# Layer A's queries and keys turned in 32 by 32 blocks by VectorE, with the quadrants moved by ScalarE, instead of by TensorE transposes

## The chip, the cores and the metric

The kernel runs on one core of a Trainium2 chip. The metric is device time in microseconds (us), from the start of the program to its end. Comparisons are made between medians of several runs. The profile is of one further execution, with every engine's instructions recorded. Its engines are PE (TensorE, matmuls) with PEld (its weight loads), DVE (VectorE), ACT (ScalarE), POOL (GpSimd) and SP (SyncE, which issues the weight loads from memory).

## The reference

Two layers over 256 tokens of width 2048, all in float32. Layer A (the first) is the one concerned:

```
xn   = rms_norm(h, norm_attn[0]);  mem_n = rms_norm(mem, norm_mem[0])
proj = xn @ w_in_a[0]                       # 12 heads of q, k, v, then 4 heads of qm, 128 wide each
q = rms_norm(split_heads(proj[q part], 12), qk_gain_a[0, 0])     # norm over each head's 128
k = rms_norm(split_heads(proj[k part], 12), qk_gain_a[0, 1])
v = split_heads(proj[v part], 12)
y_main = chunk_band_attention(q, k, v, rel_bias[0])              # softmax over the band, with bias
y_mem  = memory_attention(split_heads(proj[qm part], 4), mem_n, w_mem_kv[0], ...)
h = h + concat(y_main, y_mem) @ w_o[0]
h = h + square(relu(rms_norm(h, norm_mlp[0]) @ w_mlp_in[0])) @ w_mlp_out[0]
```

Layer B uses stick-breaking attention in place of the band attention, and is not touched. Scores are products of queries and keys over the 128 of a head, so both must lie with those 128 on the partitions, while the norm over a head is a sum along the 128 for each token.

## The kernel before

**Products in two parts.** Every weight is split into a high part `hi`, rounded to PE's fast float32 format, and a rest `lo`; activations are split in the same way. A product is three matmuls: hi by hi, hi by lo, lo by hi. The weights come as a `stream` of units of 128 partitions by 1024. For each unit SP loads `raw` (L250), ACT casts it to `hi` (L170), and DVE subtracts to get `lo` (L173). The pools hold 6 raw, 4 hi and 5 lo buffers. `weights` (L254) keeps `AHEAD` = 3 further units prepared in the code's order, so a unit's cast stands in the code three units before its matmuls.

**Layer A's projections.** `tokens_major` (L314) makes 512 columns of a projection for all 256 tokens, in two accumulator banks, one for each half of 128 tokens. It goes through 8 weight units of 12 matmuls (`tile_by_tokens`, L291), and the matmul's output has tokens on the partitions. There are ten such calls in layer A (L1203 to L1222): qm, the queries of the memory attention, and then for each of three groups of four heads the queries q, the keys k and the values v.

**Slots and side work.** Attention runs beside the projections. After each unit, `slot` (L271) advances a clock and lets each active generator take one step; a `yield` ends a step. `queue_side` (L268) puts a generator into a first-in first-out line, from which `slot` starts one at the earliest 5 slots after it was queued and `gap` slots after the one before it. Only PE's instructions are kept in the order of the code (`InOrder`, L64), with a few pinned ones; the other engines' instructions are ordered by the framework's scheduler, and each engine then executes its own in that order.

**What makes a normed query or key.** When the eighth unit is through, `normed_heads` (L553) is called. For each half of the tokens `half` (L556) squares the bank on ACT (L558), sums over each head on DVE (L560, L564), takes the inverse root on POOL (L568), and multiplies on DVE into `qn` (L570), a tile of 128 tokens by four heads of 128. After `wait` = 2 slots a side generator turns it: for each half, one slot apart, four PE transposes of 128x128 into a PSUM tile `tp` (L586), and one ACT activation of 128x512 (L589) that multiplies by the gain, one factor per partition, and writes the half's 128 columns of each head in `dst`.

**Who reads it.** `mem_head` (L641) multiplies queries by memory keys into `s` (L646), takes a softmax on ACT and DVE, transposes the probabilities on PE into `tp`, copies them on ACT to `pt` (L628), multiplies with the values into `yp`, and splits the result (L470, L471). `band_head` (L664) loads a bias on SP's queue and fills a corner of it on POOL, and one slot later does the same with q and k of its own group. Four memory heads are queued after qm with a gap of 4, and four band heads after each k group with a gap of 2, 2 and 1 (L1206, L1216).

Of the kernel before, what the change touches and what calls it, by code (L numbers as in the profile page):

```python
# [9 lines left out]
F32 = mybir.dt.float32  # L10
F32R = mybir.dt.float32r
AF = mybir.ActivationFunctionType
# [4 lines left out]
P = 128  # L17
D = 2048
T = 256
# [3 lines left out]
HD = 128  # L23
# [9 lines left out]
G_QK = 7 * 16  # L33
# [69 lines left out]
def trunk(  # L103
# [17 lines left out]
    nc = Engines(tc)  # L121
# [7 lines left out]
    wide = ctx.enter_context(tc.tile_pool(name="wide", bufs=7))  # L129
# [15 lines left out]
    sm = const.tile([P, N_SMALL], F32, name="sm")  # L145
# [115 lines left out]
    waiting = deque()  # L261
    active = []
    clock = {"slot": 0, "last": -99}
# [1 line left out]
    def start_side(g):  # L265
        active.append(g)

    def queue_side(g, gap):  # L268
        waiting.append((g, gap, clock["slot"] + 5))

    def slot():  # L271
        clock["slot"] += 1
        if waiting and clock["slot"] >= max(clock["last"] + waiting[0][1], waiting[0][2]):
            active.append(waiting.popleft()[0])
            clock["last"] = clock["slot"]
        for g in list(active):
            try:
                next(g)
            except StopIteration:
                active.remove(g)  # L280
# [28 lines left out]
    def unit_by_tokens(banks, act, half):  # L309
        unit = weights()  # L310
        for k2 in range(2):
            tile_by_tokens(banks, act, unit, k2, 2 * half + k2)

    def tokens_major(act, evacuate):  # L314

        banks = [ps_mm.tile([P, 512], F32, name="acc", tag="acc") for _ in range(2)]
        width["last"] = "wide"
        for half in range(8):
            unit_by_tokens(banks, act, half)
            if half == 7:  # L320
                evacuate(banks)
            slot()
# [227 lines left out]
        nc.vector.reciprocal(r2[:], r2[:])  # L550
        return r2

    def normed_heads(banks, eps_ms, gain, dst, wait=2):  # L553


        def half(m):  # L556
            sq = wide.tile([P, 512], F32, name="sqw", tag="wide")
            nc.scalar.activation(sq[:], banks[m][:], AF.Square)  # L558
            ss = tiny.tile([P, 4], F32, name="ss", tag="t4", bufs=8)
            nc.vector.tensor_reduce(  # L560
                ss[:], sq[:].rearrange("p (h d) -> p h d", d=HD), AX.X, ALU.add
            )
            ms = tiny.tile([P, 4], F32, name="msq", tag="t4", bufs=8)
            nc.vector.tensor_scalar(  # L564
                ms[:], ss[:], 1.0 / HD, eps_ms[:, 2 * m : 2 * m + 1], op0=ALU.mult, op1=ALU.add
            )
            s = tiny.tile([P, 4], F32, name="sroot", tag="t4", bufs=8)
            nc.gpsimd.tensor_tensor(s[:], ms[:], neg_half[:], op=ALU.pow)  # L568
            qn = wide.tile([P, 512], F32, name="qn", tag="wide")
            nc.vector.tensor_tensor(  # L570
                qn[:].rearrange("p (h d) -> p h d", d=HD),
                banks[m][:].rearrange("p (h d) -> p h d", d=HD),
                s[:].unsqueeze(2).to_broadcast([P, 4, HD]),
                op=ALU.mult,
            )
            return qn

        def side():
            qns = [half(0), half(1)]
            for _ in range(wait):  # L580
                yield
            for m in range(2):
                yield
                tp = ps_t.tile([P, 512], F32, name="tp", tag="t")
                for j in range(4):
                    nc.tensor.transpose(  # L586
                        tp[:, j * P : (j + 1) * P], qns[m][:, j * P : (j + 1) * P], ident[:]
                    )
                nc.scalar.activation(  # L589
                    dst.rearrange("p (h t) -> p h t", t=T)[:, :, m * P : (m + 1) * P],  # L590
                    tp[:].rearrange("p (h t) -> p h t", t=P),
                    AF.Copy,
                    scale=gain,
                )

        g = side()
        next(g)
        start_side(g)
# [42 lines left out]
    def mem_head(qm, km, vm, j, y, lag):  # L641
        s = ps_s.tile([P, 512], F32, name="s", tag="s")
        k = km[:, j * T : (j + 1) * T]
        for m in range(2):
            q = qm[:, j * T + m * P : j * T + (m + 1) * P]
            mm(s[:, m * T : (m + 1) * T], q, k, True, True)  # L646
        nmax = tiny.tile([P, 2], F32, name="nmax", tag="t2", bufs=8)
        nc.vector.tensor_reduce(
            nmax[:], s[:].rearrange("p (m k) -> p m k", k=T), AX.X, ALU.max, negate=True
        )  # L650
        p = wide.tile([P, 512], F32, name="p", tag="wide")
        sums = tiny.tile([P, 2], F32, name="sums", tag="t2", bufs=8)
        for m in range(2):
            nc.scalar.activation(
                p[:, m * T : (m + 1) * T], s[:, m * T : (m + 1) * T], AF.Exp,
                bias=nmax[:, m : m + 1], accum_out=sums[:, m : m + 1],
            )
        rs = tiny.tile([P, 2], F32, name="rs", tag="t2", bufs=8)
        nc.vector.reciprocal(rs[:], sums[:])
        for _ in range(lag):  # L660
            yield
        yield from soft_tail(p, [(0, T), (T, 2 * T)], rs, vm, j, y, NH + j, None, lag)

    def band_head(qt, kt_, vt, j, head, y, ready, lag):  # L664
        bias = nar.tile([P, T], F32, name="bias", tag="bias", bufs=6)
        nc.sync.dma_start(
            bias[:],
            bass.AP(tensor=rel.tensor, offset=rel.offset + head * REL + 129, ap=[[1, P], [1, T]]),
        )
        nc.gpsimd.memset(bias[0:64, 0:64], MASKED)  # L670
        yield
        s = ps_s.tile([P, 512], F32, name="s", tag="s")
        q0 = qt[:, j * T : j * T + P]
        q1 = qt[:, j * T + P : (j + 1) * T]
        mm(s[:, 0:P], q0, kt_[:, j * T : j * T + P], True, True)
        mm(s[:, P : P + T], q1, kt_[:, j * T : (j + 1) * T], True, True)
        ns = wide.tile([P, 512], F32, name="ns", tag="wide")
        nmax = tiny.tile([P, 2], F32, name="nmax", tag="t2", bufs=8)
        for m, (lo, hi) in enumerate([(0, P), (P, P + T)]):
            n = hi - lo  # L680
            nc.vector.tensor_tensor_reduce(
                out=ns[:, lo:hi], in0=s[:, lo:hi], in1=bias[:, n - 1 :: -1] if n < T else bias[:, ::-1],
                scale=-1.0, scalar=-MASKED, op0=ALU.add, op1=ALU.min,
                accum_out=nmax[:, m : m + 1],
            )
        p = ns
        sums = tiny.tile([P, 2], F32, name="sums", tag="t2", bufs=8)
        for m, (lo, hi) in enumerate([(0, P), (P, P + T)]):
            nc.scalar.activation(
                p[:, lo:hi], ns[:, lo:hi], AF.Exp, bias=nmax[:, m : m + 1], scale=-1.0,  # L690
                accum_out=sums[:, m : m + 1],
            )
        rs = tiny.tile([P, 2], F32, name="rs", tag="t2", bufs=8)
        nc.vector.reciprocal(rs[:], sums[:])
        for _ in range(lag):
            yield
        yield from soft_tail(p, [(0, P), (P, P + T)], rs, vt, j, y, head, ready, lag)
# [190 lines left out]
    gq = const.tile([P, 3], F32, name="gq")  # L888
# [8 lines left out]
    mstat = {}  # L897
    xg = None
# [8 lines left out]
    km, vm = [], []  # L907

    for l, mg in enumerate((mg0, mg1)):
        if l == 1:  # L910
            xg = new_act("xg")
# [3 lines left out]
        k_ = heads4(f"km{l}")  # L915
        km.append(k_)
        vm.append(heads4(f"vm{l}"))
        g = G_QK + 2 * (1 + l) + 1
# [281 lines left out]

    start_side(x_stat_side())
    qm = heads4("qm0")
    tokens_major(xg, lambda b: normed_heads(b, mstat["xem"], gq[:, 1:2], qm[:]))  # L1203
    y = new_act("y0")
    for j in range(NM):
        queue_side(mem_head(qm, km[0], vm[0], j, y, 2), 4)  # L1206

    for i in range(3):
        q_, k_, v_ = heads4(f"q{i}"), heads4(f"k{i}"), heads4(f"v{i}")
        tokens_major(xg, lambda b: normed_heads(b, mstat["xem"], gq[:, 0:1], q_[:]))  # L1210
        tokens_major(
            xg, lambda b: normed_heads(b, mstat["xem"], sm[:, G_QK + 1 : G_QK + 2], k_[:])
        )
        ready = {}
        for j in range(4):
            queue_side(band_head(q_, k_, v_, j, 4 * i + j, y, ready, 1), 2 if i < 2 else 1)  # L1216

        def values(b, v_=v_, ready=ready):
            value_heads(b, mstat["xr"], v_)
            ready["v"] = clock["slot"] + 2  # L1220

        tokens_major(xg, values)  # L1222
# [4 lines left out]
    h = stored(x_t, "h")  # L1227
# [39 lines left out]
    for g in range(3):  # L1267
        v_ = heads4(f"vb{g}")
# [9 lines left out]
    qm = heads4("qm1")  # L1278
# [8 lines left out]
    y = new_act("y1")  # L1287
    for hd in range(NH):
# [5 lines left out]
        if hd in (1, 3, 5, 7):  # L1294
            j = hd // 2
# [77 lines left out]
```

## Time and profile before

| | |
|---|---|
| median of 3 runs | 2173.99 us (2173.0 to 2174.17) |
| the profiled execution's own time | 2172.29 us |
| its span, first to last instruction | 2170.6 us |
| PE busy | 2163.3 us (100%) |
| DVE busy | 1632.8 us (75%) |
| ACT busy | 1191.5 us (55%) |
| POOL busy | 323.8 us (15%) |
| HBM traffic | 190 GB/s over the span |

The span runs from the first instruction to the last; the program's own time is 1.7 us longer. Matmuls are pipelined, so an instruction's duration on PE is longer than the time it takes from PE: the distance from one to the next is what counts, and the chain of waits gives it. The chain is followed back from the last instruction, at each step to what released it or to the instruction before it on the same engine. Layer A's ten projections lie between 96 and 344 us of the span.

### The profile page before, as it was taken

The page shows a single profiled execution, that of the slowest core. Times are in us where ns is not written, and L with a number is a line of the kernel's source. Part 1 is how long each engine was busy: PE and PEld are TensorE (multiplying, and loading weights), DVE is VectorE, ACT ScalarE, POOL GpSimd, SP SyncE. Part 2 cuts the span into 40 slices and gives each one's busy share as a digit, 9 for nine tenths or more (in the row PEclk, how much of TensorE's full clock was granted, in tenths as well). Part 3 has the DMA queues.
Part 4 walks back from the last instruction along what each step waited for, and adds up shares of the span by engine and source line. Part 5 has one row for each costly group of instructions (what it writes and reads, how often), then busy time and mean ns, then how long its engine had stood idle before and what let it go on. Part 6 is the DMA issues. An engine that isn't in the chain of part 4 may idle for free.

```text
span 2170.6 us, 30186 instructions
## 1 busy us (share of the span) xinstructions
PE 2163.3 (100%) x11126; PEld 1856.3 (86%) x11126; DVE 1632.8 (75%) x2227; ACT 1191.5 (55%) x1670; POOL 323.8 (15%) x349
## 2 busy tenths in 40 slices
PE   9999999999999999999999999999999999999999
PEld 8888888888888888888878888888888888988887
DVE  7765555677977987997886556567797798799785
ACT  7745445555655565555545447655565556555552
POOL 0010102621001001001050112253100100100100
PEclk9999999999999999999999999999999999999999
DMA  9655656655765766666666654455676577566664
GB/s 328 196 175 161 179 173 197 187 193 166 211 215 170 209 212 184 190 215 191 200 184 185 185 193 137 128 185 185 184 202 221 167 201 225 187 179 217 190 183 151
DMA packets 213315, 414.64 MB, mean 191 GB/s; under 512 B 13232, under 2 KB 144304, under 8 KB 213168
## 3 DMA queue, kind: packets, MB, share of 16 engines
q1 hardware_dynamic: 212592, 410.63, 62.5%
q8 instruction: 87, 1.43, 0.3%
q10 hardware_dynamic: 576, 2.10, 0.3%
q14 instruction: 60, 0.49, 0.1%
HBM read 410.58 MB, written 2.10 MB: 190 GB/s over the span
## 4 chain that ended last, share of the span: by engine, by line
PE 99%; DVE 0%; ACT 0%; issue 0%; ACTq 0%
PE acc L74 94%; PE accs L74 1%; PE tp L74 1%; PE yp L74 1%; PE s L74 1%; PE z L74 1%; PE cold L74 0%; DVE lo L247 0%; ACT hi L170 0%; DVE h L980 0%; DVE lo L173 0%; DVE kvx L462 0%; ACT hi L246 0%; PE stat L74 0%; PE inv L74 0%
## 5 line engine op out<-in xcount | busy, mean ns | idle before, releaser
L173 DVE TENSOR_TENSOR lo<-raw,hi 128x1024 fp32r<-128x1024 f32 (+1 forms) x524 | 644.2, 1237 | 358.6 <-ACT hi L170 240.6
L170 ACT CAST hi<-raw 128x1024 fp32r<-128x1024 f32 (+1 forms) x524 | 546.7, 1045 | 380.7 <-PE acc L74 308.8
L74 PE MATMUL acc<-hi,hid 128*128 128x512 f32 x1484 | 484.5, 390 | 0.0
L74 PE MATMUL acc<-mlpx,hi 128*128 128x512 f32 x2048 | 472.6, 390 | 0.0
L74 PEld LDWEIGHTS acc<-mlpx,hi 128*128 128x128 f32 x2048 | 382.0, 188 | 77.8
L74 PEld LDWEIGHTS acc<-hi,hid 128*128 128x128 f32 x1484 | 278.5, 188 | 57.8
L74 PE MATMUL acc<-lo,hid 128*128 128x512 f32 x742 | 288.7, 389 | 0.0
L1077 POOL TENSOR_TENSOR hid<-upsq,hid 128x256 fp32r<-128x256 f32 x128 | 122.0, 962 | 1086.5 <-ACT hid L1076 1086.5
L224 ACT CAST hi<-raw 128x1024 fp32r<-128x1024 f32 x200 | 188.4, 946 | 137.0 <-PE acc L74 61.5
L74 PEld LDWEIGHTS acc<-mlpx,lo 128*128 128x128 f32 x2048 | 250.6, 192 | 2.8
L74 PE MATMUL acc<-mlpx,lo 128*128 128x256 f32 x2048 | 252.0, 283 | 0.0
L225 DVE TENSOR_TENSOR lo<-raw,hi 128x1024 fp32r<-128x1024 f32 x200 | 218.7, 1107 | 33.2 <-ACT hi L224 31.5
L246 ACT CAST hi<-raw 128x1024 fp32r<-128x1024 f32 x148 | 156.1, 1054 | 128.4 <-PE acc L74 108.6
L74 PE MATMUL acc<-hi,xg 128*128 128x512 f32 x640 | 210.5, 399 | 0.0
L247 DVE TENSOR_TENSOR lo<-raw,hi 128x1024 fp32r<-128x1024 f32 x148 | 182.1, 1230 | 17.9 <-ACT hi L246 17.2
L74 PEld LDWEIGHTS acc<-lo,hid 128*128 128x128 f32 x742 | 139.3, 188 | 28.8
L74 PEld LDWEIGHTS acc<-hi,xg 128*128 128x128 f32 x640 | 120.2, 188 | 24.6
L448 ACT COPY low<-acc 128x256 f32<-128x256 f32 x188 | 68.9, 366 | 112.1 <-PE acc L74 111.7
L74 PE MATMUL acc<-lo,xg 128*128 128x512 f32 x320 | 124.7, 390 | 0.0
L74 PE MATMUL acc<-y,hi 128*128 128x512 f32 x512 | 119.9, 391 | 0.0
L74 PEld LDWEIGHTS acc<-y,hi 128*128 128x128 f32 x512 | 95.0, 188 | 19.0
L1076 ACT CAST hid<-upsq 128x256 fp32r<-128x256 f32 x128 | 51.8, 406 | 76.9 <-DVE upsq L1075 76.9
(198 smaller groups left out, 2553.3 us busy)
## 6 DMA issues: line engine op xcount, KB each, us to landing
raw<-in_w_up SPq DMA_DIRECT2D x256, 512.0 KB, 4.4
raw<-in_w_down SPq DMA_DIRECT2D x256, 512.0 KB, 5.7
raw<-in_w_in SPq DMA_DIRECT2D x80, 512.0 KB, 3.6
raw<-in_w_o SPq DMA_DIRECT2D x64, 512.0 KB, 3.8
raw<-in_w_mem SPq DMA_DIRECT2D x28, 512.0 KB, 5.9
raw<-in_w_kv_v SPq DMA_DIRECT2D x24, 512.0 KB, 3.7
raw<-in_w_kv_k SPq DMA_DIRECT2D x24, 512.0 KB, 4.2
raw<-in_w_q SPq DMA_DIRECT2D x24, 512.0 KB, 4.0
```

The costliest lines, as they stand in the source:

```text
L74: return self._tc.keep_in_program_order(fn(*args, **kwargs))
L170: nc.scalar.copy(hi[:, :n], raw[:, :n])
L173: nc.vector.tensor_tensor(lo, raw, hi.bitcast(F32), op=ALU.subtract)
L224: nc.scalar.copy(hi4, src)
L225: nc.vector.tensor_tensor(lo4, src, hi4.bitcast(F32), op=ALU.subtract)
L246: nc.scalar.copy(hi4, turned)
L247: nc.vector.tensor_tensor(lo4, turned, hi4.bitcast(F32), op=ALU.subtract)
L448: nc.scalar.copy(low[:], bank[:, T:])
L1076: nc.scalar.copy(hid[:, f, :T], a[:])
L1077: nc.gpsimd.tensor_tensor(hid[:, f, T:], a[:], hid[:, f, :T].bitcast(F32), op=ALU.subtract)
```

## The change

For qm, the three q groups and the first two k groups, the eight PE transposes and the two activations of `normed_heads` are replaced. DVE's transposition turns each 32 by 32 block of a 128x512 tile in place: block row a (32 tokens) and block column b (32 of a head's 128) stay where they are, and only the inside of the block is turned. ACT then moves block row a, column b of all four heads to partitions 32b and columns 32a of the half, with the gain, in one activation of 32 partitions by 4 x 32 elements. That makes 16 activations for each half, 32 for each group, and a step ends after every eight. The third k group, and the calls for the memory keys and for layer B, keep PE's transposes.

The memory heads of layer A and the band heads of groups 0 and 1 now start 7 slots after they are queued at the earliest, and those of group 2 still 5.

```
-    def queue_side(g, gap):
-        waiting.append((g, gap, clock["slot"] + 5))
+    def queue_side(g, gap, first=5):
+        waiting.append((g, gap, clock["slot"] + first))
...
-    def normed_heads(banks, eps_ms, gain, dst, wait=2):
+    def quadrants(turned, m, gain, dst):
+        src = turned.rearrange("p (h d) -> p h d", d=HD)
+        dst = dst.rearrange("p (h t) -> p h t", t=T)
+        for a in range(4):
+            for b in range(4):
+                nc.scalar.activation(
+                    dst[32 * b : 32 * b + 32, :, m * P + 32 * a : m * P + 32 * a + 32],
+                    src[32 * a : 32 * a + 32, :, 32 * b : 32 * b + 32],
+                    AF.Copy, scale=gain[32 * b : 32 * b + 32],
+                )
+            if a % 2 == 1:
+                yield
+
+    def normed_heads(banks, eps_ms, gain, dst, wait=2, blocks=False):
...
             for _ in range(wait):
                 yield
+            if blocks:
+                for m in range(2):
+                    xt = wide.tile([P, 512], F32, name="xt", tag="wide")
+                    nc.vector.transpose(xt[:], qns[m][:])
+                    yield from quadrants(xt[:], m, gain, dst)
+                return
             for m in range(2):
                 yield
                 tp = ps_t.tile([P, 512], F32, name="tp", tag="t")
...
-    tokens_major(xg, lambda b: normed_heads(b, mstat["xem"], gq[:, 1:2], qm[:]))
+    tokens_major(xg, lambda b: normed_heads(b, mstat["xem"], gq[:, 1:2], qm[:], blocks=True))
...
-        queue_side(mem_head(qm, km[0], vm[0], j, y, 2), 4)
+        queue_side(mem_head(qm, km[0], vm[0], j, y, 2), 4, 7)
...
-        tokens_major(xg, lambda b: normed_heads(b, mstat["xem"], gq[:, 0:1], q_[:]))
-        tokens_major(
-            xg, lambda b: normed_heads(b, mstat["xem"], sm[:, G_QK + 1 : G_QK + 2], k_[:])
-        )
+        tokens_major(xg, lambda b: normed_heads(b, mstat["xem"], gq[:, 0:1], q_[:], blocks=True))
+
+        k_gain = sm[:, G_QK + 1 : G_QK + 2]
+        tokens_major(xg, lambda b: normed_heads(b, mstat["xem"], k_gain, k_[:], blocks=i < 2))
...
-            queue_side(band_head(q_, k_, v_, j, 4 * i + j, y, ready, 1), 2 if i < 2 else 1)
+            queue_side(band_head(q_, k_, v_, j, 4 * i + j, y, ready, 1), *((2, 7) if i < 2 else (1,)))
```

## The prediction

> **What bounds the kernel now.** I read the page first, then the chain of waits through layer A's projections, then the timelines of ACT (ScalarE) and DVE (VectorE) there.
>
> ```profile
> span 2170.6 us, 30186 instructions
> PE 2163.3 (100%) x11126; PEld 1856.3 (86%) x11126; DVE 1632.8 (75%) x2227; ACT 1191.5 (55%) x1670; POOL 323.8 (15%) x349
> ...
> PE 99%; DVE 0%; ACT 0%; issue 0%; ACTq 0%
> ```
>
> PE (TensorE) is 99% of the chain, so an instruction that leaves PE shortens the run by what it holds the chain for, if nothing then makes PE wait. In the next fence, from the chain between 85 and 330 us, the columns are start, length, what and how many.
>
> ```profile
> 85.05 27.24 PE acc L74 x120
> 112.29 0.34 PE stat L74 x4
> 112.63 11.00 PE acc L74 x48
> 123.63 0.44 PE tp L74 x4
> 124.06 2.77 PE acc L74 x12
> 126.83 0.44 PE tp L74 x4
> 127.27 5.49 PE acc L74 x24
> 132.76 0.86 PE s L74 x4
> ...
> 144.55 0.44 PE tp L74 x4
> 144.99 0.87 PE s L74 x4
> ...
> 151.83 0.86 PE yp L74 x4
> ...
> 229.41 0.44 PE tp L74 x4
> 229.84 2.77 PE acc L74 x12
> 232.61 0.44 PE tp L74 x4
> 233.05 19.09 PE acc L74 x84
> ```
>
> The reader should see that PE never waits here. 120 projection matmuls take 27.24 us, so one weight unit (12 matmuls) takes 2.72 us. A burst of four transposes holds the chain for 0.44 us, 0.11 each.
>
> ```profile
> L173 DVE TENSOR_TENSOR lo<-raw,hi 128x1024 fp32r<-128x1024 f32 x71 | 86.9, 1224 | 67.4 <-ACT hi L170 67.2
> L170 ACT CAST hi<-raw 128x1024 fp32r<-128x1024 f32 x71 | 74.6, 1051 | 92.9 <-PE acc L74 60.3 <-issue 29.9 <-ACT ns L689 1.8
> L74 PE MATMUL tp<-ident,qn 128*128 128x128 f32 x48 | 7.2, 272 | 0.0
> L589 ACT ACTIVATE q<-tp,gq 128x512 f32<-128x512 f32 x6 | 4.1, 683 | 0.0
> ```
>
> These rows are the groups by line, shapes apart, from 100 to 320 us. The 48 transposes are exactly those that the change removes (six groups of eight). The row of hi says why ACT matters: each weight unit needs one cast of 1.05 us, followed by one DVE subtraction of 1.22 us, and the cast waits for PE to free a hi buffer.
>
> **The change part by part.**
>
> *PE.* Twelve bursts of 0.44 us go: 5.28 us. In each group both bursts are followed by slower matmuls: 2.77 us for the next 12 against 2.72, and 19.09 us for the next 84 against 84/120 x 27.24 = 19.07, or 5.49 for 24 against 5.45. That is 0.05 to 0.09 us per group beyond the first unit's 0.05, so about 0.1 us per group and 0.6 us for six. I count it, since it sits right behind the bursts; its ends are 0 and 0.6. PE saving: 5.9 us (5.3 to 5.9).
>
> *DVE.* Each half gains one transposition of 128x512 f32 from SBUF to SBUF; the trace has none. A plain DVE instruction of that size takes 0.69 us (the qn row below); the dearest elementwise one, the reciprocal, takes 1.75 us for 256 columns, 3.5 us for 512.
>
> ```profile
> L550 DVE RECIPROCAL r_mlp<-r_mlp 128x256 f32<-128x256 f32 x2 | 3.5, 1753 | 0.1
> ...
> 223.00:246.00 23.00, 23.00 (x107) 19.03 (x106) 12.70 (x15) 10.69 (x12) 2.98 (x2) 1.00 0.63 174
> ```
>
> I take 0.69, because nothing is computed on the element. DVE is busy 12.70 of 23 us in a stage with one group (second line, busy time by window, DVE's figure in the third place), so 1.4 us more fits. At 3.5 us it would start the next step later (a rival).
>
> *ACT.* Two activations of 0.68 us leave each group, and 32 activations of 32 partitions by 128 elements come. All partitions run side by side, so the size that counts is 128 elements. The nearest row is the exponential over 128 elements with a per-partition operand:
>
> ```profile
> 190.03 0.40 ACT L689 ACTIVATE ns<-ns,nmax 128x128 f32<-128x128 f32 x1
> 190.34 0.19 ACT L689 ACTIVATION_READ_ACCUMULATOR ns<-ns,nmax 128x1 f32 x1
> ```
>
> It takes 0.40 us, and the next instruction starts 0.31 us after it, since neighbours on ACT overlap. The bounds are 0.31 and, if short pieces do not overlap, 0.40. I take 0.31, the pitch that the row shows: 32 x 0.31 = 9.9 us per group against 1.2 to 1.4 before. ACT is busy 10.69 of 23 us in the same stage, so the sum fits, but the 32 come bunched. Whether they delay the casts decides the result.
>
> The Trainium skill, "ScalarE: Activation LUTs", section "What ACT_TABLE_LOAD costs", gives 280 ns + 0.833 ns per element with one pointer operand and 93 ns of overlap between neighbours, so an estimate of 0.29 us of pitch. By that figure the 32 would take 9.4 us, and the stall worked out below would vanish.
>
> *When the casts are due.* The rows of one group (qm) on ACT, then on DVE:
>
> ```profile
> 118.22 1.05 ACT L170 CAST hi<-raw 128x1024 fp32r<-128x1024 f32 x1
> 119.17 0.59 ACT L558 ACTIVATE sqw<-acc 128x512 f32<-128x512 f32 x1
> 120.94 1.05 ACT L170 CAST hi<-raw 128x1024 fp32r<-128x1024 f32 x1 [1.18 <-PE acc L74]
> 123.66 1.05 ACT L170 CAST hi<-raw 128x1024 fp32r<-128x1024 f32 x1 [1.67 <-PE acc L74]
> 124.62 0.68 ACT L589 ACTIVATE qm<-tp,gq 128x512 f32<-128x512 f32 x1
> ```
>
> ```profile
> 120.45 0.68 DVE L570 TENSOR_TENSOR qn<-acc,sroot 128x512 f32<-128x512 f32 x1
> 121.05 0.67 DVE L560 TENSOR_REDUCE ss<-sqw 128x4 f32<-128x512 f32 x1
> 121.76 0.23 DVE L564 TENSOR_SCALAR msq<-ss,em_x 128x4 f32<-128x4 f32 x1
> 122.03 1.22 DVE L173 TENSOR_TENSOR lo<-raw,hi 128x1024 fp32r<-128x1024 f32 x1
> ```
>
> Count from the group's end, 118.22. Casts come at 0, 2.72, 5.44, 8.17 and 10.9 us. The hi pool has four buffers, so each cast serves the unit that starts 8.17 us later. Less 1.05 for the cast, 1.22 for the subtraction and about 0.1 for handovers, plus one matmul (27.24/120 = 0.23), because lo enters at a unit's second step, a cast may start 6.0 us late before PE waits. It holds its place from 0.96 us on (123.66 to 124.62).
>
> The code issues eight pieces per slot, one slot per unit, and the first half's piece of qn is ready at 2.9. DVE is free again at 3.8, so the block transposition ends at 4.5, or at 5.6 if the subtraction goes ahead of it. Where ACT is full I assume it takes its work in program order: eight pieces, cast, eight, cast.
> Early case: 16 pieces run from 4.5 to 9.5, the cast due at 5.44 ends at 10.4, eight pieces to 12.9, the cast of 8.17 ends at 13.9, eight pieces to 16.4. The cast of 10.9 then starts 5.5 late, and PE does not wait.
> Late case: the cast of 5.44 runs first and ends at 6.4, 16 pieces to 11.4, eight more to 13.8, a cast to 14.8, eight to 17.3. The cast of 10.9 starts 6.4 late, and PE waits 0.4 us.
>
> Four groups (qm, q1, k1, q2) have no attention work on ACT beside this. For them I take half of 4 x 0.4: 0.7 us after rounding down (ends 0 and 1.6). In q0 and k0 a memory head's tail and the next one's start fall in the same slots. They add a copy and two exponentials to ACT:
>
> ```profile
> L654 ACT ACTIVATE p<-s,nmax 128x256 f32<-128x256 f32 x8 | 3.7, 470 | 4.8 <-DVE nmax L648 4.8
> L628 ACT COPY pt<-tp 128x512 f32<-128x512 f32 x4 | 2.3, 581 | 0.0
> ```
>
> That is about 0.58 + 2 x 0.47 = 1.5 us, but the same head work gives PE 0.44 + 0.87 + 0.86 = 2.2 us (rows from 144.55 to 151.83), which moves the due times back by more. I count no stall there.
>
> *The head starts moved by two slots.* The memory heads of layer A and band groups 0 and 1 start two slots later. That costs PE nothing while other matmuls fill the slots, and the last band group keeps its start, so the layer's tail is not lengthened. With each band head its bias load on SP's queue and its fill on POOL move too, past two weight loads that wait for neither; I count them at nothing. The first reader of a turned tile is s of the first memory head: at 132.76, so 14.5 us after the group's end. With two units (5.49) more and the bursts (1.0) gone, that is 19.0. The pieces end at 16.4 to 17.3, so nearly 2 us stay, and all of it would go at 0.37 us per piece. The wait of ACT for the block transposition holds the casts queued behind it, which is in the sums above.
>
> *Sum.* 5.9 - 0.7 = 5.2 us saved. The profiled execution took 2172.29 us, 1.7 beyond its span, and should become 2167.1. It lies 1.7 below the median of the runs, 2173.99, which becomes **2168.8 us**. What a measurement can tell from no change here is about 0.2%, 4.35 us: 2169.64 is the edge, and the forecast clears it by under 1 us.
>
> **The rivals.**
>
> *ACT eats part of it.* A piece at 0.34 us gives in the early case 4.5 + 32 x 0.34 + 1.9 = 17.3, a cast 6.4 late and 0.4 us of stall; in the late case 7.4 + 10.9 = 18.3, 1.4 us. Over four groups that is 1.6 to 5.6, mean 3.6, so 5.9 - 3.6 = 2.3 us saved: 2171.7. A block transposition of 3.5 us delays the pieces' start to 7.3 and ends in the same place (7.3 + 9.9 + 0.96 = 18.2, 1.3 us in each of six groups, 7.8 us lost, 2175.9). For it: the rows have no 32-partition piece and no DVE transposition. Against: no row of 128 elements shows a pitch above 0.31.
>
> *ACT becomes the bound, slower.* If short pieces do not overlap, each costs 0.40 us. The cast of 10.9 then starts at 4.5 + 12.8 + 1.9 = 19.2, 8.3 late, a stall of 2.3 us in the early case and 3.3 in the late. The readers s of qm would wait as well, but for the same lost time. Six groups at 2.8 us are 17 us lost, 11 net: 2185. It decides from a stall of 10.3/6 = 1.7 us per group, about 0.37 us a piece between the cases. Against it: every pair of neighbours on ACT in the rows above overlaps. The Trainium skill, "VectorE: DVE Perf Modes", section "Rules for kernel authors", speaks for this side: it sends a 128x128 transpose to TensorE where PSUM will do as its target.
>
> *PE transposes cost their full length.* If each gave back its 272 ns, PE would gain 48 x 0.272 = 13.1 us: 2160.9. Against it stands the 0.44 us for four in the chain. The Trainium skill, "TensorE: Matmul & The Clock Gate", section "Part 4: PE-mode transpose", gives about 275 ns in one kernel's context. The trace agrees with it as a duration, but not as time taken from PE.
>
> **How the numbers follow.** Forecast 0.50; partly eaten 0.34; ACT the bound 0.14; full length 0.02. The forecast lies from 2168.1 (5.9 saved) to 2169.6. The range starts at 2167.2: the saving in full, less 0.9, most of the 1.2 us between the slowest and the fastest of the three runs. It reaches to 2177.0, past the slow block transposition, so that it leaves out the full-length case and the slower one, 0.16. Faster by over 0.2%: 0.50 + 0.02 = 0.52. Within: 0.34. Slower: 0.14.
>
> **What would show it.** After the change the tp<-ident,qn row should count 48 fewer transposes and the chain in layer A should lose the 0.44 pieces. The pieces on ACT should start 0.31 us apart, and the block transposition should take about 0.7 us on DVE. Casts from 5 to 17 us after a group's end should start up to 6 us late, without a gap in PE. PE waiting for lo or hi in units 5 to 8 after a group, above all in qm, q1, k1 and q2, is the partly eaten case; gaps of 2 us or more in every group are the slower one. The forecast is wrong if ACT's order is not the code's, for instance if pieces stand ahead of an earlier cast while they wait for DVE.

## The result and the profile after

The changed kernel takes **2201.48 us** (median, 2201.21 to 2203.32) beside 2173.49 us for the kernel before: ratio 1.0133, 95% interval 1.0121 to 1.0145. It is 28.0 us slower, where 5.2 us faster was forecast and 2177.0 was the upper end of the range.

The page of the changed kernel, in the lines that answer to those shown of before:

```profile
span 2199.5 us, 30272 instructions
PE 2171.4 (99%) x11078; PEld 1857.4 (84%) x11078; DVE 1637.1 (74%) x2239; ACT 1259.3 (57%) x1850; POOL 321.8 (15%) x349
...
PE 94%; ACT 4%; DVE 1%; issue 1%; POOL 0%; POOLq 0%; ACTq 0%
```

The 48 transposes have gone from PE (11126 instructions to 11078). ACT has come into the chain with 4%: PE now waits. For what it waits in layer A's projections (from here on, "layer A" means this stretch), from the view of waits between 96 and 345 us (in all, times, longest):

```profile
PE acc L74 <- ACT hi L170: 13.6, 6, 3.0
PE acc L74 <- DVE lo L173: 4.8, 7, 0.8
PE yp L74 <- ACT pt L650: 3.1, 2, 1.6
```

These are six waits for a cast, one in each of the six groups, and seven for the subtraction that follows a cast. One group (qm) shows how it comes to that. First ACT, then DVE, in order of time; the group ends at about 118.06:

```profile
118.06 1.05 ACT L170 CAST hi<-raw 128x1024 fp32r<-128x1024 f32 x1
119.02 0.59 ACT L574 ACTIVATE sqw<-acc 128x512 f32<-128x512 f32 x1
120.78 1.06 ACT L170 CAST hi<-raw 128x1024 fp32r<-128x1024 f32 x1 [1.17 <-PE acc L74]
123.50 1.06 ACT L170 CAST hi<-raw 128x1024 fp32r<-128x1024 f32 x1 [1.66 <-PE acc L74]
125.34 9.88 ACT L560 ACTIVATE qm<-xt,gq 32x128 f32<-32x128 f32 x24 [0.78 <-DVE xt L601]
135.25 1.04 ACT L170 CAST hi<-raw 128x1024 fp32r<-128x1024 f32 x1
136.31 3.27 ACT L560 ACTIVATE qm<-xt,gq 32x128 f32<-32x128 f32 x8
139.60 2.94 ACT L170 CAST hi<-raw 128x1024 fp32r<-128x1024 f32 x3
```

```profile
124.00 0.69 DVE L586 TENSOR_TENSOR qn<-acc,sroot 128x512 f32<-128x512 f32 x1 [0.90 <-POOL sroot L584]
124.61 1.29 DVE L601 STREAM_TRANSPOSE xt<-qn 128x512 f32<-128x512 f32 x2
```

Three things are to be read here. 24 pieces take 9.88 us, so 0.41 from one to the next: each piece takes its 0.40 whole and nothing overlaps. They start 7.3 us after the group's end, because the first block transposition stands behind the second half's qn on DVE, and that qn waits 0.90 us for its inverse root on POOL. And 24 of them stand ahead of a cast that was due at 8.17 us after the group's end and now starts at 17.2, 9.0 late. What that does to PE shows in busy time by window (the second figure is PE's busy time, then the number of its instructions; PEclk is the third figure from the end):

```profile
118.00:134.00 16.00, 16.00 (x73) 13.20 (x71) 7.80 (x11) 12.06 (x25) 3.00 (x2) 1.00 0.41 134
134.00:136.30 2.30, 0.35 (x2) 0.00 (x0) 0.00 (x0) 2.24 (x4) 0.00 (x0) 1.00 0.00 0
136.30:137.60 1.30, 0.74 (x1) 0.24 (x1) 1.23 (x1) 1.25 (x4) 0.00 (x0) 0.55 0.00 0
137.60:142.60 5.00, 5.00 (x12) 3.94 (x13) 1.92 (x2) 4.87 (x8) 0.00 (x0) 0.50 0.40 108
```

PE stands still at 134 and again at 136.3. Three matmuls in a row start at 133.96, 136.34 and 137.60; less the usual 0.227 us for each of the two steps, that is 3.2 us in all. Then PE runs for 5 us at a granted clock of 0.50. Eleven matmuls take 5.06 us there (chain, from 137.60), where 11 x 0.227 = 2.5 was usual.

### The profile page after: what moved, and what is told of

It is laid out like the page before. It is cut to its first block, busy times and chain, and to the rows that moved or that the text cites. A ratio compares the mean times of both kernels' runs of the same rounds, so it can differ in the third digit from the quotient of the medians.

```text
span 2199.5 us, 30272 instructions
## 1 busy us (share of the span) xinstructions
PE 2171.4 (99%) x11078; PEld 1857.4 (84%) x11078; DVE 1637.1 (74%) x2239; ACT 1259.3 (57%) x1850; POOL 321.8 (15%) x349
## 4 chain that ended last, share of the span: by engine, by line
PE 94%; ACT 4%; DVE 1%; issue 1%; POOL 0%; POOLq 0%; ACTq 0%
PE acc L74 90%; ACT q L560 1%; PE accs L74 1%; ACT k L560 1%; PE yp L74 1%; PE tp L74 1%; DVE lo L173 1%; PE z L74 1%; ACT hi L170 1%; PE s L74 1%; ACT qm L560 0%; POOL sroot L584 0%; DVE qn L586 0%; PE cold L74 0%; DVE xt L601 0%
## 5 line engine op out<-in xcount | busy, mean ns | idle before, releaser
L74 PE MATMUL acc<-hi,xg 128*128 128x512 f32 x640 | 215.2, 409 | 13.6 <-ACT hi L170 13.6
L74 PE MATMUL acc<-lo,xg 128*128 128x512 f32 x320 | 129.1, 403 | 4.8 <-DVE lo L173 4.8
```

What stands on the lines that cost most here:

```text
L74: return self._tc.keep_in_program_order(fn(*args, **kwargs))
```

## The experiments

Theory: the loss comes from the pieces on ScalarE, which hold up the casts. Rivals: the block transpositions on VectorE, the later starts of the attention heads, or the drop of PE's clock.

**What each part is worth.** Two activations in place of the 32 pieces:

```
-        for a in range(4):
-            for b in range(4):
-                nc.scalar.activation(dst[32*b.., :, m*P + 32*a..], src[32*a.., :, 32*b..], ..., scale=gain[32*b..])
+        nc.scalar.activation(dst[:, :, m * P : (m + 1) * P], src, AF.Copy, scale=gain)
```

> As the change, but each half is moved by one activation of 128x512 instead of 16 small ones, so the quadrants stay in the wrong place: it leaves that part of the turning out and keeps the block transposition, the missing TensorE transposes and the later head starts. If the small activations on ScalarE make the whole loss: about 5.9 us faster than before, 2167.6, and no gap on PE in layer A. If the block transpositions on VectorE or the later head starts have a part in it: above 2174.

Measured: 2169.34 us beside 2173.42, ratio 0.9982 (0.9972 to 0.9991). No wait for hi or lo is left, so the block transpositions on VectorE, which this run keeps, do not hold up a cast; two waits of 1.56 us for a pt are left. The same with the heads at 5 slots:

> The kernel with one activation of 128x512 per half (quadrants not moved), and the heads at their old 5 slots. It gives the gain of the missing transposes alone. If the prediction's term is right: 5.9 us faster than before, 2167.6. If the two waits of 1.56 us that the run with later heads still shows were its whole difference to that: 2166.3. If a transpose was worth its whole 272 ns: 2160.

Measured: 2165.97 us beside 2172.48, ratio 0.9968 (0.9956 to 0.9980), and PE never waits in layer A. So the missing transposes are worth 6.5 us, and the later heads cost 6.5 - 4.1 = 2.4 (the two medians lie 3.4 apart, and the two waits make 3.1). What is left of the change is 28.0 + 4.1 = 32.1 us for the pieces, 5.4 for each group.

The later heads alone, in the kernel before (`queue_side(..., 4, 7)` and `(2, 7)` for the first two band groups):

> The kernel before with nothing but the later start of the heads (7 slots instead of 5). If the start costs nothing, as the prediction had it: within 1 us of before. If it takes part in the loss: 2 us slower or more.

Measured: 2180.49 us, ratio 1.0032 (1.0021 to 1.0043), 7.1 slower. "Costs PE nothing" was wrong. The waits of that run, from its view of waits:

```profile
PE yp L74 <- ACT pt L628: 3.1, 2, 1.6
...
PE tp L74 <- ACT pt L628: 2.4, 2, 1.2
```

Two slots later a memory head's transposes meet the group's own in the one tp bank, and a band head's pt stands on ACT behind the squares of the next group and a cast. The two rows make 5.5 us. In the profiled execution another 1.7 lie outside this stretch: from 1119.0 us on PE's granted clock is 0.50 for 3.4 us, behind a wait of 1.9 us. The kernel before has that wait as well, and its clock stays at 1.00.

**Why a piece takes 0.41.** Each group gets another form:

```
 "stay":    dst[32*a.., :, 32*b..] <- src[32*a.., :, 32*b..]      # q0: same partitions, four in a row
 "all":     dst[:, :, 32*a..]      <- src[:, :, 32*a..]           # k0: 128 partitions
 "number":  as the change, scale=1.0                              # q1
 "gain_in": as the change, scale=gain[32*a..]                     # k1
 "dense":   as the change, 128 neighbouring elements              # q2
```

> Each of the six groups gets another form of the small activation, and the trace gives the distance between neighbours for each. qm: as in the change. q0: the 32 partitions stay where they are, output on the input's partitions (so the quadrants are not moved). k0: eight activations of all 128 partitions by 128 elements, no move. q1: as in the change, but multiplied by the number 1 instead of the gain. k1: as in the change, but the gain is read from the input's partitions. q2: as in the change in partitions, but 128 neighbouring elements in and out. All but qm leave out or misplace part of the layout. Theory 1 (crossing partitions stops neighbours from overlapping): qm, q1, k1, q2 at 0.41 us or near it (q1 0.1 less), q0 and k0 at 0.31. Theory 2 (fewer than 128 partitions stop it): q0 at 0.41 as well, k0 alone at 0.31. Theory 3 (the gain's address on other partitions than the input): k1, q0, q1 and k0 at 0.31, qm and q2 at 0.41. Theory 4 (the pieces of 32 elements): q2 alone at 0.31. Theory 5 (a small activation with a factor per partition simply costs 0.41): all but q1 at 0.41.

ACT of that run in order of time, one line for each form (qm, q0, k0, q1, k1, q2):

```profile
125.68 9.86 ACT L576 ACTIVATE qm<-xt,gq 32x128 f32<-32x128 f32 x24 [0.78 <-DVE xt L613]
...
155.99 7.71 ACT L576 ACTIVATE q<-xt,gq 32x128 f32<-32x128 f32 x24 [0.30 <-DVE xt L613]
...
183.39 2.45 ACT L576 ACTIVATE k<-xt,sm 128x128 f32<-128x128 f32 x8 [0.30 <-DVE xt L613]
...
233.07 10.21 ACT L576 ACTIVATE q<-xt 32x128 f32<-32x128 f32 x32 [0.75 <-DVE xt L613]
...
264.06 9.87 ACT L576 ACTIVATE k<-xt,sm 32x128 f32<-32x128 f32 x24 [0.78 <-DVE xt L613]
...
317.77 8.22 ACT L576 ACTIVATE q<-xt,gq 32x128 f32<-32x128 f32 x20 [0.75 <-DVE xt L613]
```

The stretch less the last piece's own length, divided by the number of steps, gives the distance from one piece to the next: 0.41, 0.32, 0.29, 0.32, 0.41 and 0.41. The number 1 only shortens a piece, from 0.40 to 0.31; it does not make it overlap. Theory 1 (a piece that writes to other partitions than it reads does not overlap) fits. But "stay" also kept its partitions for four pieces in a row, so it leaves open which of the two counts. The next run parts the two:

```
 "stay" now with the partitions changing at every piece (q0, k1);  four in a row with one output range (k0, q2)
 "pairs": two pieces of 64 elements on the same pair of ranges, then the next pair (q1)
```

> More forms of the small activation, told apart by the distance between neighbours. qm: as in the change. q0: input and output on the same partitions, but other partitions at every instruction. q1: two activations of 64 elements in a row on the same pair of partition ranges, then the next pair. k0 and q2: as in the change, ordered so that four in a row have the same output partitions. k1: as q0. q0 and k1 leave the move out. Theory 1a (an activation whose output lies on other partitions than its input does not overlap with the next): q0 and k1 at 0.31, k0 and q2 at 0.41, q1 at 0.36 throughout. Theory 1b (neighbours overlap only if both use the same partitions): q0, k1, k0 and q2 at 0.41, q1 at 0.36 and 0.27 in turn, 0.31 in the mean. Theory 1c (only a change of the output's partitions stops it): k0 and q2 at 0.31 in three of four, q0 and k1 at 0.41.

```profile
257.25 5.47 ACT L568 ACTIVATE q<-xt,gq 32x64 f32<-32x64 f32 x16
...
286.48 13.13 ACT L568 ACTIVATE k<-xt,sm 32x128 f32<-32x128 f32 x32
```

"stay" with a change at every piece is at 0.41 (13.13 for 32), and so is one output range with changing inputs. Of the pairs, only those on the diagonal overlap (the first starts at 257.25 and 257.50); the crossing ones follow at 0.36, their whole length. None of the three theories holds alone. Neighbours overlapped only where both had the same partitions for input and output, and kept them. None of the change's pieces has such a neighbour.

**Is the length of a piece the whole cause?** Fewer and longer pieces, both halves in one (16 of 256 elements):

```
+            dst[32*b.., (both m), :, 32*a..] <- src[32*a.., (both m), :, 32*b..]      # yield after every 4
```

> The change in everything but the size of the pieces: one activation moves a quadrant for both halves of the tokens, 16 of 32 partitions by 256 elements for each group instead of 32 by 128, four to a slot. At 0.41 + 128 x 0.833 ns = 0.51 us without overlap that is 8.2 us of ScalarE for each group instead of 13.2. If the late casts are the loss, the waits for hi and lo go, the two waits of later heads (3.1 us) stay beside a saving of 5 to 6, and the time is 2170 to 2172. If the loss hangs on something else that came with the block transposition: above 2185.

Measured: 2180.77 us, ratio 1.0037 (1.0023 to 1.0051). The work fell from 13.2 to 8.3 us for each group, but the kernel is still 8.3 us slower than before, where 2170 to 2172 was expected. Its ACT:

```profile
126.53 7.78 ACT L558 ACTIVATE qm<-xt,gq 32x256 f32<-32x256 f32 x15 [1.24 <-DVE xt L599]
134.33 1.05 ACT L170 CAST hi<-raw 128x1024 fp32r<-128x1024 f32 x1
```

The code has 4 pieces to a slot; 15 of the 16 stand in a row. The next run has the pitch that the prediction worked with (`scale=1.0`, which leaves out the gain):

> The change with the number 1 in place of the gain (so the gain is left out): the small activations then take 0.31 us from start to start, the value that the prediction worked with. It asks whether the forecast fails by that value alone. If it does: no wait for hi and lo, and 2169 to 2171 (6.5 saved, 2.4 lost to the later heads). If the pieces' late start (7.3 us after the group's end, where the prediction had 4.5 to 5.6) and their order are a second cause: after 24 pieces the cast of 8.17 starts at 7.3 + 7.4 = 14.7, 6.6 late, 0.6 us lost in each group, 2173; and if all 32 stand ahead of it, as they did for one group in the run with mixed forms, 17.2, 9.1 late, 3 us lost in each, 2187.

Measured: 2181.83 us, ratio 1.0041 (1.0027 to 1.0054), between the 2173 and the 2187 of the expectation. The group's end is at 117.71:

```profile
124.99 7.66 ACT L560 ACTIVATE qm<-xt 32x128 f32<-32x128 f32 x24 [0.78 <-DVE xt L601]
132.67 1.05 ACT L170 CAST hi<-raw 128x1024 fp32r<-128x1024 f32 x1
```

The cast stands behind 24 pieces and starts 6.8 us late, and in some groups it and later ones still make PE wait. At 0.31 a piece the forecast fails too, but 18.8 us less are lost than with the change. Then each block transposition directly behind its qn:

> As the run with the number 1, and each half's block transposition stands in the code directly behind its qn, so that the first half's pieces can start 4.5 us after the group's end, as the prediction had it (the gain is left out again). If the start is the second cause: 24 pieces end at 11.9, the cast of 8.17 is 3.8 late, no wait, 2169 to 2171. If the order is (all 32 ahead of that cast): 14.4, 6.3 late, 0.3 us in each group, 2171 to 2173. If the start does not matter: the same time as with the number 1 alone.

Measured: 2184.89 us, ratio 1.0053 (1.0038 to 1.0069), more than without it, which no theory expected. In layer A PE waits for no hi and no lo any more in that run, but for this:

```profile
PE yp L74 <- ACT pt L652: 14.3, 2, 7.1
```

```profile
225.01 5.07 ACT L560 ACTIVATE q<-xt 32x128 f32<-32x128 f32 x16
230.10 0.48 ACT L652 COPY pt<-tp 128x384 f32<-128x384 f32 x1
```

The pieces, early now, stand ahead of the last band head's pt, for which PE waits 7.13 us. That head reaches q1's start only because it begins two slots later. Hence the last of this series, `2 if i < 2 else 1` for the band heads:

> The prediction's own conditions put together: 0.31 us for a piece (the number 1, the gain left out), the first half's pieces from 4.5 us after the group's end, and the band heads at their old 5 slots (the memory heads at 7). The run with the same pieces and the band heads at 7 slots had no wait for hi or lo, and two of 7.13 us of a band head for its pt. If the forecast fails by these three points alone: 6.5 saved less at most 3 of late readers, 2166 to 2169. If something else is in it: 2172 or more.

Measured: 2169.57 us, ratio 0.9986 (0.9976 to 0.9996), 3.2 faster than before and just above the expected range. Waits of 0.55, 1.91 and 0.36 us are left, for k and for yp's bank. Its ACT in qm, where the group's end is at 118.02:

```profile
122.18 5.08 ACT L560 ACTIVATE qm<-xt 32x128 f32<-32x128 f32 x16
127.28 2.00 ACT L170 CAST hi<-raw 128x1024 fp32r<-128x1024 f32 x2
129.19 5.09 ACT L560 ACTIVATE qm<-xt 32x128 f32<-32x128 f32 x16
134.31 3.89 ACT L170 CAST hi<-raw 128x1024 fp32r<-128x1024 f32 x4
```

The order is not that of the code here either, for 16 pieces stand in a row twice. But they start at 4.2 us, and the cast due at 10.9 starts 5.4 late, inside the 6.0 that are free. So with the short pitch and the early start this order costs PE nothing.

**Amount or order?** The wide pieces, two to a slot over eight slots, their readers at 12 slots:

> The wide pieces (16 of 32 partitions by 256 elements, 0.52 us each), but two to a slot over eight slots instead of four to a slot, and the heads that read them start at 12 slots. The same work on ScalarE: 8.3 us for each group. If the bunching is what costs, and not the amount: each slot has 1.05 + 1.04 of 2.72 us, no cast is late, and the time is 2166 to 2169, depending on what the later heads meet. If the amount is: as with four to a slot, 2180.

Measured: 2186.02 us, ratio 1.0061 (1.0047 to 1.0075). The run says nothing on amount or order, for its ACT again shows 15 in a row:

```profile
126.16 7.78 ACT L558 ACTIVATE qm<-xt,gq 32x256 f32<-32x256 f32 x15 [1.25 <-DVE xt L599]
```

The slots of the code order PE only. The order on ACT is the scheduler's; that it places a piece as soon as its input is ready by its own estimate would fit, but is not shown. So the order has to be held there as well. Both runs spread the pieces over eight slots, two wide ones or four small ones to a slot, and begin two slots later in the code (wide) or one (small):

```
-        nc.scalar.copy(hi[:, :n], raw[:, :n])
+        pin(nc.scalar.copy(hi[:, :n], raw[:, :n]), weave["on"])     # on from qm to the third k
-            nc.scalar.activation(dst[32*b.., ...], src[32*a.., ...], ...)
+            pin(nc.scalar.activation(dst[32*b.., ...], src[32*a.., ...], ...))
```

> As the run that spread the wide pieces over eight slots in the code, but now the order is held on ScalarE too: in layer A the casts and the pieces are executed in the order of the code, two pieces (1.04 us) between two casts. Theory 1 (the loss comes from the order, a bunch of pieces ahead of a cast that is ready): no wait for hi or lo is left and PE's waits shrink to what the later heads make, 2166 to 2171. Theory 2 (the loss comes from the amount, 8.3 us on ScalarE for each group): about 2186, as without the order held.

> The change's own pieces, 32 of 0.41 us with the gain, with the order held: four pieces (1.65 us) between two casts over eight slots, heads at 12 slots. Together with the cast that is 2.6 to 2.7 us in a slot of 2.72, and squares and heads come on top. Theory 1 (order): most of the change's 32 us are gone, 2168 to 2180, the rest from the slots that overflow. Theory 2 (amount): above 2195, as the change.

Measured: with the wide pieces **2165.58 us** beside 2172.80, ratio 0.9965 (0.9952 to 0.9978), and PE waits for nothing in layer A. With the change's own 32 pieces 2170.99 us, ratio 0.9991 (0.9982 to 1.0000). ACT of the latter:

```profile
127.74 1.64 ACT L562 ACTIVATE qm<-xt,gq 32x128 f32<-32x128 f32 x4
129.40 1.05 ACT L172 CAST hi<-raw 128x1024 fp32r<-128x1024 f32 x1
130.47 1.63 ACT L562 ACTIVATE qm<-xt,gq 32x128 f32<-32x128 f32 x4
```

The same pieces at the same 0.41 us, the same casts, and about 30 us less than the change. The first piece of qm starts 7.1 us after the group's end, no earlier than in the change. The heads start at 12 slots here instead of 7; in the run before (wide pieces, order not held) that did not help. The order that was held is four pieces to a cast. The prediction's own, eight to a cast, was not run at this pitch. A part of what separates it from the wide version are waits of 2.28 us for a lo and three near 0.45 for a pt.

**The clock.** In each group 16 added matmuls on data that is there, one slot ahead of PE's gap:

```
+                for _ in range(16):
+                    mm(spare[:], xg[:, 0, :P], xg[:, 0, :], True, True)
```

> The change, with 16 further matmuls of 128x128 by 128x512 (about 3.6 us) on data that is there, into a bank that nobody reads, one slot before the unit at which PE stood still. Theory 1 (after an idle stretch of 2 us and more PE runs at half its clock for some us, and that is a part of the loss): the added matmuls lie in time that was idle, the slow matmuls behind the gaps go, and the run is about 10 us shorter, 2190, in spite of the added work. Theory 2 (the slow matmuls come from something else, such as ScalarE's and VectorE's work at that moment): the slow matmuls stay, and the time is 2201 or longer.

Measured: 2200.29 us, ratio 1.0122 (1.0105 to 1.0139). The slow matmuls go but for 3.4 us in q0, and the time stays. Busy time of qm by window, columns as above:

```profile
138.00:143.00 5.00, 4.83 (x22) 3.74 (x21) 1.92 (x2) 4.93 (x9) 0.00 (x0) 1.00 0.32 105
```

The clock is 1.00 where it was 0.50, ACT is as full as before (4.93 of 5.00), and 22 matmuls fit in place of 12, but 16 x 0.227 = 3.6 us went into the filling, more than the 3.2 that PE had stood still. In q0 the run also waits 3.0 us for a pt. So the expected 10 us did not come.

What the half clock costs in the change can be estimated from its own trace. These are all the stretches of layer A in which the granted clock was 0.50, one in each group but q1:

```profile
136.43:143.26 6.83, 6.31 (x14) 4.62 (x15) 3.48 (x3) 6.56 (x12) 0.00 (x0) 0.50 0.35 85
173.97:177.38 3.41, 3.41 (x9) 2.66 (x9) 3.41 (x4) 3.06 (x8) 0.00 (x0) 0.50 0.80 181
204.69:208.10 3.41, 3.35 (x8) 2.67 (x9) 3.41 (x5) 2.34 (x3) 0.00 (x0) 0.50 0.67 181
286.61:290.02 3.41, 3.41 (x9) 2.63 (x10) 0.51 (x1) 3.33 (x7) 0.00 (x0) 0.50 0.52 154
341.23:344.64 3.41, 3.41 (x9) 2.63 (x9) 1.41 (x2) 3.36 (x6) 0.00 (x0) 0.50 0.53 154
```

PE is busy for 19.9 us in them, and at the full clock would need half, so an estimate is 10 of the 32.1 us. The waits for hi and lo make 18.4 more. The run with the filling fits that: over six groups it adds 96 x 0.227 = 21.8 us of matmuls, PE's waits in layer A fall from 21.5 to 9.0, and the time at half clock falls from 20.5 to 3.4, worth 8.5; that makes 0.8 us more, beside 1.2 less between the two medians. How long a PE at full clock would have waited for the next late cast instead is not shown.

**Another way.** VectorE can write a turned block straight to another quadrant, so ACT can be left alone for the queries:

```
+            nc.vector.transpose(dst[32*b.., (both m), :, 32*a..], src[32*a.., (both m), :, 32*b..])    # 16 a group
```

> Another way to the same aim, correct to the reference: the queries (qm, q0 to q2) are turned by VectorE alone, 16 block transpositions of 32 partitions by 256 elements that write straight to the quadrant's place, without ScalarE; the queries' gain is multiplied into the keys' gain, all keys keep TensorE's transposes, the band heads start at 5 slots and the memory heads at 8 with gaps 3, 2 and 4. Four groups less on TensorE are worth 4 x 0.98 = 3.9 us: 2169.6, if VectorE takes 0.35 us or less for a piece and no unit's lo is 6 us late. If a piece takes 0.7 us (the same as one of 128x512), VectorE has 11 us more in each group, lo comes late, and it is slower than 2174.

> The version that VectorE turns alone (16 pieces of 32 by 256, straight to the quadrant), correct to the reference, with layer B's memory queries turned in the same way too. One group more at 0.98 us: 2166.6, if layer B's VectorE has room. If it has not (it is busier there): 2168 or more.

Measured: 2167.59 us beside 2172.48, ratio 0.9976 (0.9967 to 0.9986), and with layer B's memory queries 2166.83 beside 2172.64, ratio 0.9971 (0.9961 to 0.9982). PE does not wait in layer A in either. A piece takes 0.44 us, more than the 0.35 allowed, and still fits:

```profile
L562 DVE STREAM_TRANSPOSE q<-qn 32x256 f32<-32x256 f32 x48 | 20.9, 436 | 0.8
```

The woven wide pieces and the two direct versions beat both kernels. They lie about 2 us apart and come from different series, so which is the fastest is not shown.

## Why the prediction was wrong

**PE: right in kind, a little low.** Forecast 5.9 us for the transposes (5.3 to 5.9), measured 6.5. Their full length of 272 ns (13.1 us) is excluded.

**DVE: right.** Forecast 0.69 us for a block transposition of 128x512, measured 0.685.

**"I take 0.31, the pitch that the row shows": wrong by size.** It is 0.41. The row quoted was of neighbours that keep all 128 partitions, and the pieces change theirs each time. The Trainium skill, "ScalarE: Activation LUTs", section "What ACT_TABLE_LOAD costs", says that neighbours overlap by about 93 ns. The run with mixed forms agrees where partitions stay (pieces of 0.40 start 0.29 apart) and shows nothing of it where they change. The slower rival named this mechanism, at 0.40 a piece, and priced it at 2185, 16 us too low, for the reasons that follow.

**"Where ACT is full I assume it takes its work in program order: eight pieces, cast, eight, cast": the step that failed.** The stall of 0.7 us in the sum rests on it and on the pitch; in its place the pieces cost 32.1 us. The pieces stood 24 in a row, which the prediction had named as a sign that it would be wrong, and started at 7.3 us, not at 4.5 to 5.6. At the assumed pitch of 0.31 this made the kernel 9 us slower (number). With the order held, four pieces to a cast, the loss went in spite of the long pitch and the late start (woven). With the assumed pitch and start it went too, though the order was not the code's (number_early_5). So none of the three makes the loss alone: at the short pitch the order cost PE nothing once the start was early, and at the long pitch the loss went once the order was held. The long pitch with an early start was not run, and the 32.1 us cannot be divided among the three. A start at 7.3 stood among the rivals as well, for another reason (a slow block transposition), and was priced at 2175.9 with the order of the code. The allowance was good: 6.0 us late is free, and the cast 9.0 late cost 3.2 us of standstill.

**"That costs PE nothing": wrong by 2.4 us**, and by up to 7.1 with PE's transposes in place. I looked at the readers of the turned tiles and at the order of the queue, and not at what the moved heads' own steps meet: one tp bank, and ACT at the next group's start.

**Left out: PE's clock.** After the standstill come some matmuls at half speed, in qm 2.6 us more for eleven, by the estimate above about 10 us in all. The price of the slower rival had no such term.

With pitch, start and band heads as the prediction assumed them, 3.2 us are saved (number_early_5), so even then the forecast saving of 5.2 would have been too high by 2.

## What to carry to other kernels

When work moves to an engine that feeds the bottleneck, ask not only whether its sum fits but what stands ahead of each hand-over that is due, in the order in which that engine really executes; a step of the code is no evidence of that order unless it is held. Price a small instruction from a row with the same partitions on both sides as its neighbour, not just the same size. A start that is moved "where nothing waits" meets other buffers at the new place, so follow each of its steps to the bank and the engine that it shares.

## What the hardware showed that was not expected

Two of these small ACT instructions in a row overlapped by about 0.1 us only if both read and wrote the same partitions; else the next one started when the last had ended (0.41 for 0.40, 0.36 for 0.35, 0.32 for 0.31).

PE's granted clock fell to 0.50 after gaps of 2.0 to 3.0 us followed by one of 0.5 to 0.8, in five of the six groups of the changed kernel (in qm already after the first: the one matmul between the gaps took 0.74 us, 0.50 in the others); in q1 the gaps were 2.48 and 0.77 and the matmuls behind them kept their pace. The length of the gap alone did not decide: a wait of 2.28 us (woven) left the clock at 1.00, and the same wait of 1.9 us (until 1117.9 us in shift_only, 1111.3 in the kernel before) was followed by half speed in the first alone. The Trainium skill, "TensorE: Matmul & The Clock Gate", section "Why this matters for your kernels", warns of idle gaps beyond about 3 us between matmul bursts; here shorter ones did it.

A block transposition of 32 partitions wrote to another range of 32 partitions in the same instruction, 0.44 us for 256 float32 elements.
